# A two-layer hybrid recurrent backbone: the first layer's modulation starts in the mLSTM stage instead of HGRN2, and its weights come through GpSimd's DMA queue

## The chip, the cores and the metric

The kernel runs on one core of one Trainium2 chip. A core has TensorE (PE; its weight loads are a row of their own, PEld), VectorE (DVE), ScalarE (ACT), GpSimd (POOL) and SyncE (SP); the last two here mostly issue transfers or stand idle. The metric is device time in microseconds (us) of one execution; less is better. Times of several runs are given by their median.

## The reference, cut to what matters

Two layers run over 256 context tokens and 1024 latent tokens of width 1024, all in float32. What the change touches is the modulation: a product of one vector per token kind (latent `c`, context `c_ctx`) with a 1024 x 6144 matrix per layer, whose six pieces shift, scale and gate the two sub-layers.

```python
for layer in range(DEPTH):
    mod_l = (jax.nn.silu(c) @ w_ada[layer] + b_ada[layer])[:, None, :]
    mod_c = (jax.nn.silu(c_ctx) @ w_ada[layer] + b_ada[layer])[None, None, :]
    sh1_l, sc1_l, g1_l, sh2_l, sc2_l, g2_l = jnp.split(mod_l, 6, axis=-1)
    sh1_c, sc1_c, g1_c, sh2_c, sc2_c, g2_c = jnp.split(mod_c, 6, axis=-1)
    pl = split_proj(modulate(xl, sh1_l, sc1_l) @ w_in[layer])
    pc = split_proj(modulate(xc, sh1_c, sc1_c) @ w_in[layer])
    mixed = (hgrn2_mixer(pc, pl, lb_all[layer]),
             mlstm_mixer(pc, pl, ml_gate_bias[layer]),
             retention_mixer(pc, pl, rt_decay_logit[layer], rot),
             gla_mixer(pc, pl, gla_w_a[layer], gla_b_a[layer]))
    ...
    xl = xl + g1_l * mixer_out(raw_l, pl, g_heads[layer], w_out[layer])
    xl = xl + g2_l * sq_relu_mlp(modulate(xl, sh2_l, sc2_l), w_ff1[layer], w_ff2[layer])
```

The pieces `sh1` and `sc1` are needed first; `g1`, `sh2`, `sc2` and `g2` only from the output projection on.

## The kernel before

**Stages.** A layer is: the norm and the first projections; the mixers (method `mixers`) in the order GLA, HGRN2 (two pairs of heads), mLSTM (two pairs), retention (two pairs); the output projection (`outproj`); the MLP (`mlp`). Every finished group of chunks of a mixer goes through `finish` (the norm of heads): a matmul at L705, and on DVE the multiplication at L708, by which the stages are told apart below.

**Dense work beside the mixers.** The input projections and gates are products of 128 x 128 weight tiles with all tokens, three matmuls each in reduced precision (L293 to L295 with the weights stationary, L631 to L633 for the values). They stand in a queue (`Fill`). `Fill.along` steps a mixer and the queue in turn by estimated cost; `Fill.until` steps the queue alone until a marked piece is done. The mixers' chains run over DVE, ACT and PE.

**The modulation.** Piece 0 of the first layer (`sh1`, `sc1`) is made at the start on PE. Pieces 1 and 2 come from the generator `ada_part`. It works in eight quarters per piece, each of 256 columns (W = 256). In a quarter, for each of eight slices k of the contraction, a 128 x 256 tile of weights (128 KB) is loaded into a ring of four buffers (L402), and DVE multiplies it with the k-th values of the two vectors and accumulates: L406 for k = 0, L408 for the others, so two DVE instructions per tile and 16 per quarter. Then four small matmuls per quarter (L413) sum over the partitions and DVE adds the bias (L419, and L421 where 1 is added). The two accumulators are used again in the next quarter. In all that is 128 tiles, 256 DVE instructions at L406 and L408, and 16 quarters. The second layer's modulation uses the same generator inside the first layer's MLP with W = 512; it is not changed in substance.

**What sets the order.** `Fill.step` runs the modulation along with the queue: on three of every five steps of the queue it advances the generator by one `yield`. In the kernel before, that begins when HGRN2 begins:

```python
for cost in gen:
    self.n += 1
    if self.also and self.n % 5 in (0, 2, 4):
        next(self.also, None)
    return cost
```

The program is then laid out per engine by a scheduler that may move instructions; each engine runs its own list in order. All loads and stores of this stage, the modulation's weights too, are issued by SP. GpSimd has a few memsets to do (L767, L1289, L1290).

Of the kernel before, what the change touches and what calls it, by code (L numbers as in the profile page):

```python
# [42 lines left out]
class Ring:  # L43
# [4 lines left out]
    def next(self):  # L48
        x = self.items[self.i % len(self.items)]
        self.i += 1  # L50
        return x
# [146 lines left out]
class K:  # L198
# [189 lines left out]
            m = self.mod[:, l, a:a + 8, :]  # L388
            nc.vector.tensor_scalar(m, m, 1.0, None, op0=ALU.add)

    def ada_part(self, l, r, toks, wring, tmp, acc, banks, W):


        nc = self.nc
        one = self.m64[:, 1:2]
        nt, nb = len(toks), W // 128
        for q in range(2048 // W):
            g, h = divmod(q * W, 512)
            A = [b(W) for b in acc[:nt]]
            for k in range(NK):  # L400
                w = wring.next()(W)
                nc.sync.dma_start(w, self.io["w_ada"][l, r, k, :, g, h:h + W])  # L402
                for i, j in enumerate(toks):
                    c = self.cc[:, k, j:j + 1]
                    if k == 0:
                        nc.vector.tensor_scalar(A[i], w, c, None, op0=ALU.mult)  # L406
                    else:
                        nc.vector.scalar_tensor_tensor(A[i], w, c, A[i], op0=ALU.mult, op1=ALU.add)  # L408
                yield
            ps = self.bank(banks().next())  # L410
            for i in range(nt):
                for cb in range(nb):
                    nc.tensor.matmul(ps[:, 2 * cb + i:2 * cb + i + 1], lhsT=A[i][:, 128 * cb:128 * cb + 128], rhs=one,  # L413
                                     start=True, stop=True)
            o = 16 * r + nb * q
            mo = self.mod[:, l, o:o + nb, toks[0]:toks[0] + nt]
            bb = self.bada[:, l, o:o + nb].unsqueeze(2).to_broadcast([128, nb, nt])
            v = ps[:, 0:2 * nb].rearrange("p (c j) -> p c j", j=2)[:, :, 0:nt]
            nc.vector.tensor_tensor(mo, v, bb, op=ALU.add)  # L419
            if (r == 0 and g >= 2) or (r == 2 and g < 2):  # L420
                nc.vector.tensor_scalar(mo, mo, 1.0, None, op0=ALU.add)  # L421
            yield
# [997 lines left out]
    def mixers(self, l, ada):  # L1420
        nc, hp = self.nc, self.heap

        fill = Fill(5)
        sp = self.sp
        gl = self.gl
        gq = [self.copyT(gl, "K", GLK, TBS, 32 ** -0.5), self.copyT(gl, "Q", GLQ, self.otbs)]
        for g in gq:
            g.pre(2)
        m = fill.add(*gq)
        self.turn(sp)  # L1430
        rows = self.ml_rows(sp["sp"])
        next(rows)
        hg = [{"p": p} for p in range(2)]
        ml = [{"p": p} for p in range(2)]
        rt = [{"p": p} for p in range(2)]

        def share(a, b, *names):
            for x in names:
                if x in a:
                    b[x] = a[x]  # L1440

        def ml_dense(p):
            return [self.spill(MLK + p, TBS, 0.125), self.spill(MLQ + p, self.otbs)]


        fill.along(self.feat_gl(gl, sp["sp"]), 1.0)
        hp.free(sp["sp"])
        fill.add(*self.spill_hg(0))
        fill.until(m)
        next(rows, None)  # L1450
        m = fill.add(self.feat_v(0, hg[0]))
        fill.along(self.mix_vec(gl, "gl"), RATIO[0])
        m1 = fill.add(*self.spill_hg(1))
        fill.until(m)

        ao = hp.alloc(1536, True) if l == 0 else None
        if l == 0:
            fill.also = ada([ao.sub(256 * i, 256) for i in range(6)], lambda: self.dbanks)
        self.feat_hg(hg[0])
        share(hg[0], hg[1], "V")  # L1460
        fill.add(*(self.gate(6 + p, GLG + p, True) for p in range(2)))
        fill.along(self.mix_vec(hg[0], "hg"), RATIO[1])
        fill.add(*ml_dense(0))
        fill.until(m1)
        self.feat_hg(hg[1])
        m = fill.add(self.spill_v(1))
        fill.add(self.gate(0, HGG, False), *ml_dense(1))
        fill.along(self.mix_vec(hg[1], "hg"), RATIO[2], fill.done + len(fill.q) - 2)
        hp.free(hg[0]["V"])
        fill.until(m)  # L1470

        V = self.get(ml[0], "V65")(NC, 260)
        for c in range(0, NC, 5):
            nc.sync.dma_start(V[:, c:c + 5, :], self.d_v[:, c:c + 5, :])
        share(ml[0], ml[1], "V65")
        self.rt_setup()
        for p in range(2):
            self.fetch(ml[p], "K", MLK + p, TBS)
            self.fetch(ml[p], "Q", MLQ + p, self.otbs)
            if p == 0:  # L1480
                m = fill.add(self.feat_v(2, rt[0]))
                fill.add(self.gate(1, HGG + 1, False))
            else:
                m = fill.add(*self.feat_rt(rt[0]))
                fill.add(self.gate(2, MLO, False))
            fill.along(self.mix_ml(ml[p]), RATIO[3])
            fill.until(m)
        hp.free(ml[0]["V65"], self.mlN_o, self.mlAE_o)

        share(rt[0], rt[1], "V")  # L1490
        m = fill.add(*self.feat_rt(rt[1]))
        self.rt_tables()
        fill.along(self.mix_rt(rt[0]), RATIO[4])
        last = fill.add(self.gate(3, MLO + 1, False))
        fill.add(self.last_gates(((4, RTG, True), (5, RTG + 1, True))))
        fill.until(m)
        fill.along(self.mix_rt(rt[1]), RATIO[4], last)
        fill.until(10 ** 9)
        if l == 0:
            for _ in fill.also:  # L1500
                pass
            hp.free(ao)
        for x in self.mix_pools:
            x.release()
# [66 lines left out]
def build(ctx, tc, io):  # L1571
    b = K(ctx, tc, io)
    b.setup()
    nc = b.nc
# [14 lines left out]
    for l in range(2):  # L1589
# [3 lines left out]

        def ada(bufs, banks):
            for r in (1, 2):
                yield from b.ada_part(0, r, (0, 1), Ring(bufs[:4]), None, bufs[4:6], banks, 256)
        b.mixers(l, ada)
        b.outproj(l)
        na = 3
# [3 lines left out]
        wring = Ring(cs[:nw])  # L1603
        aring = Ring(zip(cs[nw + nf::2], cs[nw + nf + 1::2]))
        def ada1(bufs, l=l):
            for r in range(3) if l == 0 else ():
                yield from b.ada_part(1, r, (0, 1) if r == 0 else (1,), Ring(bufs[:4]), None, bufs[4:6], lambda: b.banks, 512)
        tmps = b.tmps
        gen = ada1(cs[nw:nw + nf] + tmps.items[4:])

        def filler():
# [126 lines left out]
```

## Time and profile before

| | us |
|---|---|
| median of 3 runs | 3308.24 (3303.61 to 3309.18) |
| the profiled execution | 3300.05 |
| its span from first to last instruction | 3298.2 |
| TensorE busy in the span | 3215.6 (97%) |
| VectorE busy | 2121.8 (64%) |
| ScalarE busy | 1286.1 (39%) |
| GpSimd busy | 10.8 |

The share of busy time is a mean over stages; busy spans of PE are pipelined, so a PE that is busy all the time is not one at its peak. In the trace L708 ends HGRN2 near 555 us, mLSTM's first pair at 613, and retention's last group at 798 us; the output projection follows. In the second layer, which has no modulation beside its mixers, HGRN2 lies between about 2095 and 2283 us.

### The profile page before, as it was taken

The numbers are of one execution on the slowest core, as the hardware profiler recorded it, in microseconds if no ns is written. First come the engines' busy times: TensorE is split into PE (matmuls) and PEld (weight loads), VectorE is DVE, ScalarE is ACT, GpSimd is POOL, SyncE is SP. The second block draws the span as 40 slices with busy tenths as digits, with TensorE's granted clock in tenths as the row PEclk, the third lists the DMA queues.
The fourth block names the chain that finished last, engine by engine and source line by source line (L and its number), as shares of the span: only waits on it lengthen the run. The fifth ranks groups of instructions, "written<-read, shape, count | busy, mean of one in ns | idle before, by whom it ended". The sixth has DMA issues, their size and how long they took to land.

```text
span 3298.2 us, 52930 instructions
## 1 busy us (share of the span) xinstructions
PE 3215.6 (97%) x20936; PEld 2640.0 (80%) x20936; DVE 2121.8 (64%) x4218; ACT 1286.1 (39%) x2665; POOL 10.8 (0%) x41
## 2 busy tenths in 40 slices
PE   7998899999999999999999999999999999999998
PEld 4786688877888888888888678788778888888887
DVE  4778887787666656555655586866756555554546
ACT  4665565445322122121212565765445322222222
POOL 0000000000000000000000000000000000000000
PEclk9999899999999999999999999999999999999999
DMA  5113444434322222222211222333315111111111
GB/s 206 61 50 127 122 133 148 121 101 146 103 80 71 83 65 80 69 64 64 77 39 34 76 66 77 110 114 109 103 58 163 53 50 46 51 51 46 51 48 65
DMA packets 175010, 278.85 MB, mean 85 GB/s; under 512 B 21097, under 2 KB 66825, under 8 KB 174505
## 3 DMA queue, kind: packets, MB, share of 16 engines
q1 hardware_dynamic: 173464, 273.66, 26.5%
q8 instruction: 164, 2.69, 0.3%
q10 hardware_dynamic: 1296, 1.81, 0.2%
q14 instruction: 86, 0.70, 0.1%
HBM read 229.75 MB, written 45.64 MB: 83 GB/s over the span
## 4 chain that ended last, share of the span: by engine, by line
PE 88%; DVE 5%; DMA 3%; ACT 3%; issue 1%; SPq 0%; DVEq 0%; ACTq 0%
PE psum L293 23%; PE psum L294 23%; PE psum L295 23%; PE psum L830 2%; PE psum L600 2%; PE psum L631 2%; PE psum L633 2%; PE psum L632 1%; PE psum L817 1%; PE psum L833 1%; PE psum L1018 1%; PE psum L705 1%; PE psum L1357 1%; PE psum L413 1%; DVE px L990 1%
## 5 line engine op out<-in xcount | busy, mean ns | idle before, releaser
L525 DVE SCALAR_TENSOR_TENSOR x<-psum,st,x 128x512 f32<-128x512 f32 (+1 forms) x648 | 441.3, 690 | 213.2 <-PE psum L295 212.3
L281 ACT ACTIVATE pc<-st 128x512 fp32r<-128x512 f32 x256 | 161.2, 632 | 847.5 <-PE psum L294 808.7
L294 PE MATMUL psum<-pc,pc 128*128 128x512 f32 (+1 forms) x1296 | 475.9, 367 | 0.0
L293 PE MATMUL psum<-pc,pc 128*128 128x512 f32 (+1 forms) x1296 | 475.8, 367 | 0.0
L295 PE MATMUL psum<-pc,pc 128*128 128x512 f32 (+1 forms) x1296 | 473.8, 366 | 0.0
L293 PE MATMUL psum<-Hhi,pc 128*128 128x512 f32 (+1 forms) x1280 | 471.9, 369 | 1.7 <-ACT pc L281 1.5
L294 PE MATMUL psum<-Hlo,pc 128*128 128x512 f32 (+1 forms) x1280 | 471.9, 369 | 0.1
L295 PE MATMUL psum<-Hhi,pc 128*128 128x512 f32 (+1 forms) x1280 | 470.5, 368 | 0.0
L293 PE MATMUL psum<-Hhi,pw 128*128 128x512 f32 (+1 forms) x1192 | 451.0, 379 | 5.7 <-ACT pw L281 2.5
L295 PE MATMUL psum<-Hhi,pw 128*128 128x512 f32 (+1 forms) x1192 | 445.2, 374 | 0.0
L294 PE MATMUL psum<-Hlo,pw 128*128 128x512 f32 (+1 forms) x1192 | 444.8, 373 | 0.0
L504 DVE TENSOR_TENSOR st<-st 128x256 f32<-128x256 f32 (+1 forms) x160 | 101.8, 637 | 301.8 <-ACT pc L503 300.7
L293 PEld LDWEIGHTS psum<-pc,pc 128*128 128x128 f32 x1296 | 244.4, 189 | 43.8 <-DVE x L525 1.3
L295 PEld LDWEIGHTS psum<-pc,pc 128*128 128x128 f32 x1296 | 244.0, 188 | 43.0 <-issue 2.7
L294 PEld LDWEIGHTS psum<-pc,pc 128*128 128x128 f32 x1296 | 244.5, 189 | 41.3 <-issue 2.1
L293 PEld LDWEIGHTS psum<-Hhi,pc 128*128 128x128 f32 x1280 | 241.2, 189 | 43.5 <-ACT pc L281 2.4
L294 PEld LDWEIGHTS psum<-Hlo,pc 128*128 128x128 f32 x1280 | 241.3, 189 | 40.9 <-DVE Hlo L481 0.5
L295 PEld LDWEIGHTS psum<-Hhi,pc 128*128 128x128 f32 x1280 | 241.1, 188 | 40.9 <-DVE pc L282 0.6
L293 PEld LDWEIGHTS psum<-Hhi,pw 128*128 128x128 f32 x1192 | 226.7, 190 | 51.4 <-issue 10.1
L282 DVE TENSOR_TENSOR pc<-st,pc 128x512 fp32r<-128x512 f32 x256 | 175.5, 690 | 137.9 <-ACT pc L281 117.3
L295 PEld LDWEIGHTS psum<-Hhi,pw 128*128 128x128 f32 x1192 | 226.2, 190 | 37.6 <-issue 2.1
L294 PEld LDWEIGHTS psum<-Hlo,pw 128*128 128x128 f32 x1192 | 226.8, 190 | 36.2 <-issue 2.2
(398 smaller groups left out, 4950.4 us busy)
## 6 DMA issues: line engine op xcount, KB each, us to landing
st<-w_ff SPq DMA_DIRECT2D x256, 256.0 KB
st<-w_inT SPq DMA_DIRECT2D x96, 256.0 KB
ph<-w_ada SPq DMA_DIRECT2D x128, 128.0 KB
st<-w_out SPq DMA_DIRECT2D x50, 256.0 KB
pc<-w_ada SPq DMA_DIRECT2D x48, 256.0 KB
st<-w_ada SPq DMA_DIRECT2D x48, 256.0 KB
d_z<-st SPq DMA_DIRECT2D x40, 256.0 KB
ps<-w_ada SPq DMA_DIRECT2D x32, 256.0 KB
```

The source lines that it names most:

```text
L281: nc.scalar.activation(hi, raw, AF.Copy)
L282: (eng or nc.vector).tensor_tensor(lo, raw, F(hi), op=ALU.subtract)
L293: t.matmul(out, lhsT=w[0], rhs=m[0], start=first, stop=False)
L294: t.matmul(out, lhsT=w[0], rhs=m[1], start=False, stop=False)
L295: t.matmul(out, lhsT=w[1], rhs=m[0], start=False, stop=last)
L413: nc.tensor.matmul(ps[:, 2 * cb + i:2 * cb + i + 1], lhsT=A[i][:, 128 * cb:128 * cb + 128], rhs=one, start=True, stop=True)
L504: nc.vector.tensor_tensor(r, r, r, op=ALU.mult)
L525: nc.vector.scalar_tensor_tensor(x, ps, self.mod[:, l, 40 + o, j:j + 1], x, op0=ALU.mult, op1=ALU.add)
L600: t.matmul(ps[:, 0:304], lhsT=h[a], rhs=u[b], start=(k + i == 0), stop=(k == NK - 1 and i == 2))
L631: t.matmul(ps[:, e, :], lhsT=h[0], rhs=u[0], start=(k == 0), stop=False)
L633: t.matmul(ps[:, e, :], lhsT=h[1], rhs=u[0], start=False, stop=(k == NK - 1))
L830: nc.tensor.matmul(o, lhsT=ST[r0:r0 + kd, c, d, :], rhs=qd[d](c)[r0:r0 + kd, :], start=(j == 0), stop=False, tile_position=(r0, 0))
```

## The change

`ada_part` takes the queue on which it loads as an argument. For the first layer's pieces 1 and 2 that is now GpSimd's queue, for the second layer it stays SP's. With W = 256 the generator now yields after every second tile, so each advance issues two loads and four DVE instructions. In `mixers` the buffers are taken and the generator is started after HGRN2's second pair, just before mLSTM. An unused argument goes.

```diff
-    def ada_part(self, l, r, toks, wring, tmp, acc, banks, W):
+    def ada_part(self, l, r, toks, wring, acc, banks, W, queue):
...
                 w = wring.next()(W)
-                nc.sync.dma_start(w, self.io["w_ada"][l, r, k, :, g, h:h + W])
+                queue.dma_start(w, self.io["w_ada"][l, r, k, :, g, h:h + W])
                 for i, j in enumerate(toks):
                     c = self.cc[:, k, j:j + 1]
...
-                yield
+                if W == 512 or k % 2:
+                    yield
...
         fill.until(m)
 
-        ao = hp.alloc(1536, True) if l == 0 else None
-        if l == 0:
-            fill.also = ada([ao.sub(256 * i, 256) for i in range(6)], lambda: self.dbanks)
         self.feat_hg(hg[0])
...
         share(ml[0], ml[1], "V65")
         self.rt_setup()
+        ao = hp.alloc(1536, True) if l == 0 else None
+        if l == 0:
+            fill.also = ada([ao.sub(256 * i, 256) for i in range(6)], lambda: self.dbanks)
         for p in range(2):
...
-                yield from b.ada_part(0, r, (0, 1), Ring(bufs[:4]), None, bufs[4:6], banks, 256)
+                yield from b.ada_part(0, r, (0, 1), Ring(bufs[:4]), bufs[4:6], banks, 256, nc.gpsimd)
...
-                yield from b.ada_part(1, r, (0, 1) if r == 0 else (1,), Ring(bufs[:4]), None, bufs[4:6], lambda: b.banks, 512)
+                yield from b.ada_part(1, r, (0, 1) if r == 0 else (1,), Ring(bufs[:4]), bufs[4:6], lambda: b.banks, 512, nc.sync)
```

The lists of the two programs show where the instructions went. (After L409 the lines of the changed program are one higher: L414 there is L413 before, L420 is L419, L709 is L708, L1304 is L1303, L1290 and L1291 are L1289 and L1290.)

**DVE at the start of HGRN2.** `px` and `ph` are the two memories of the mixers; L882 to L1037 are lines of the HGRN2 mixer, L798 and L802 its chain of states. Before, just behind the L708 that ends GLA:

```order
L990 SCALAR_TENSOR_TENSOR px_0_688<-px_0_688,st 128x512
L408 SCALAR_TENSOR_TENSOR ph_0_251<-ph_0_251,st 128x256 x2
L798 SCALAR_TENSOR_TENSOR ph_0_251<-ph_0_251 128x128
L408 SCALAR_TENSOR_TENSOR ph_0_251<-ph_0_251,st 128x256
L798 SCALAR_TENSOR_TENSOR ph_0_251<-ph_0_251 128x128
L802 SCALAR_TENSOR_TENSOR ph_0_251<-ph_0_251 128x128
L798 SCALAR_TENSOR_TENSOR ph_0_251<-ph_0_251 128x128
L408 SCALAR_TENSOR_TENSOR ph_0_251<-ph_0_251,st 128x256
```

At the same place of the changed program:

```order
L310 SCALAR_TENSOR_TENSOR st<-psum,st 128x512
L723 TENSOR_TENSOR st<-st,psum 128x512
L799 SCALAR_TENSOR_TENSOR ph_0_251<-ph_0_251 128x128
L732 SCALAR_TENSOR_TENSOR st<-st 128x512
L799 SCALAR_TENSOR_TENSOR ph_0_251<-ph_0_251 128x128
L733 TENSOR_TENSOR st<-st 128x512
L799 SCALAR_TENSOR_TENSOR ph_0_251<-ph_0_251 128x128
```

The modulation's L408 is gone from between the mixer's and the dense work's instructions.

**DVE between mLSTM's first and second pair of heads.** L708 (L709 in the changed program) is the first pair's last multiplication; L1303 (L1304) scales the second pair's keys; L282 splits a weight tile, L310 and L651 belong to a gate. Before:

```order
L708 SCALAR_TENSOR_TENSOR st<-st 128x128
L1303 TENSOR_TENSOR px_0_688<-psum,st 128x3x64
L310 SCALAR_TENSOR_TENSOR st<-psum,st 128x256
L1303 TENSOR_TENSOR px_0_688<-psum,st 128x3x64
L419 TENSOR_TENSOR st<-psum,st 128x4
L406 TENSOR_SCALAR ph_0_251<-ph_0_251,st 128x256
L651 TENSOR_TENSOR st<-st 128x256
L421 TENSOR_SCALAR st<-st 128x4
L406 TENSOR_SCALAR ph_0_251<-ph_0_251,st 128x256
L408 SCALAR_TENSOR_TENSOR ph_0_251<-ph_0_251,st 128x256 x2
L798 SCALAR_TENSOR_TENSOR px_0_688<-px_0_688,ph_0_251 128x65
```

In the changed program:

```order
L709 SCALAR_TENSOR_TENSOR st<-st 128x128
L420 TENSOR_TENSOR st<-psum,st 128x4
L406 TENSOR_SCALAR ph_0_251<-ph_0_251,st 128x256 x2
L282 TENSOR_TENSOR pw_0_247<-st,pw_0_247 128x512
L408 SCALAR_TENSOR_TENSOR ph_0_251<-ph_0_251,st 128x256 x8
L1304 TENSOR_TENSOR px_0_688<-psum,st 128x3x64
L408 SCALAR_TENSOR_TENSOR ph_0_251<-ph_0_251,st 128x256 x6
L406 TENSOR_SCALAR ph_0_251<-ph_0_251,st 128x256
L420 TENSOR_TENSOR st<-psum,st 128x4
L406 TENSOR_SCALAR ph_0_251<-ph_0_251,st 128x256
L1304 TENSOR_TENSOR px_0_688<-psum,st 128x3x64
L408 SCALAR_TENSOR_TENSOR ph_0_251<-ph_0_251,st 128x256 x8
```

Before the second pair's keys are scaled, three whole quarters (48 instructions of the modulation, 24 tiles) now stand in DVE's list almost in one piece; the third goes on in the same way behind these rows.

**GpSimd's list in the first layer's mixers.** L1290 and L1291 clear the states of an mLSTM pair, L768 sets a column of ones for its values. Before (L767, L1289, L1290):

```order
L1208 MEMSET ph_0_251 128x16
L767 MEMSET st 128x4 x10
L1289 MEMSET px_0_688 128x65
L1290 MEMSET px_0_688 128x65
L1289 MEMSET px_0_688 128x65
L1290 MEMSET px_0_688 128x65
```

In the changed program:

```order
L1209 MEMSET ph_0_251 128x16
L402 DMA ph_0_251<-w_ada 128x256
L768 MEMSET st 128x4 x10
L1290 MEMSET px_0_688 128x65
L402 DMA ph_0_251<-w_ada 128x256 x4
L1291 MEMSET px_0_688 128x65
L402 DMA ph_0_251<-w_ada 128x256 x22
L1290 MEMSET px_0_688 128x65
L1291 MEMSET px_0_688 128x65
L402 DMA ph_0_251<-w_ada 128x256 x101
```

All 128 loads now stand in GpSimd's list, and some memsets behind them.

Counted over the whole DVE lists, between the multiplications that end the stretches named above (before, then changed): HGRN2 from its first group (289 to 555 us) holds 148 and 7 instructions at L406 and L408; mLSTM's first pair (555 to 613) 16 and 57; up to the second pair's first group (to 644) 14 and 67; the rest of the second pair (to 682) 16 and 34; retention's first pair (to 735) 34 and 56; up to the second pair's first group (to 779) 16 and 35; the rest 0 and 0. The other instructions of DVE in the last six stretches are 112 and 101, 58 and 64, 63 and 71, 71 and 76, 53 and 57, 22 and 20.

## Rows read from the trace of the kernel before

**Rows 1.** The page: busy us by engine; busy tenths and clock in 40 slices.

```profile
PE 3215.6 (97%) x20936; PEld 2640.0 (80%) x20936; DVE 2121.8 (64%) x4218; ACT 1286.1 (39%) x2665; POOL 10.8 (0%) x41
...
PE   7998899999999999999999999999999999999998
PEld 4786688877888888888888678788778888888887
DVE  4778887787666656555655586866756555554546
...
PEclk9999899999999999999999999999999999999999
```

**Rows 2.** Busy time by stretch: HGRN2, mLSTM, retention of layer 0; then layer 1's HGRN2.

```profile
core 0: us, PE busy (x) PEld busy (x) DVE busy (x) ACT busy (x) POOL busy (x), PEclk, DMA share, GB/s
289.00:555.00 266.00, 241.79 (x2339) 198.70 (x2337) 226.10 (x562) 154.41 (x343) 1.28 (x12) 0.94 0.41 127
555.00:613.00 58.00, 56.55 (x484) 49.94 (x483) 44.08 (x128) 27.15 (x84) 0.24 (x2) 1.00 0.44 132
613.00:644.00 31.00, 31.00 (x221) 24.10 (x219) 25.19 (x73) 15.07 (x39) 0.00 (x0) 1.00 0.48 127
644.00:682.00 38.00, 38.00 (x223) 31.06 (x224) 32.04 (x84) 19.23 (x55) 0.00 (x0) 1.00 0.28 86
682.00:735.00 53.00, 53.00 (x361) 40.48 (x360) 42.52 (x107) 21.63 (x50) 0.00 (x0) 1.00 0.36 111
735.00:779.00 44.00, 44.00 (x309) 35.59 (x309) 32.33 (x73) 16.46 (x39) 0.00 (x0) 1.00 0.18 52
779.00:798.00 19.00, 19.00 (x129) 15.05 (x128) 10.39 (x23) 11.50 (x29) 0.00 (x0) 1.00 0.45 144
...
2095.00:2283.00 188.00, 186.33 (x1876) 152.80 (x1874) 132.53 (x282) 119.12 (x251) 1.29 (x12) 1.00 0.34 109
```

**Rows 3.** The same view of L408 alone, the modulation's accumulation on DVE.

```profile
289.00:555.00 266.00, 58.38 (x131) 0.94 0.41 127
555.00:613.00 58.00, 6.30 (x14) 1.00 0.44 132
613.00:644.00 31.00, 5.59 (x12) 1.00 0.48 127
```

**Rows 4.** Stretches of 10 us in HGRN2 with a low clock.

```profile
310.00:320.00 10.00, 2.16 (x64) 1.74 (x64) 10.00 (x21) 3.43 (x7) 0.00 (x0) 0.59 0.39 128
320.00:330.00 10.00, 8.50 (x62) 6.90 (x63) 7.40 (x20) 3.98 (x7) 0.00 (x0) 0.73 0.14 44
360.00:370.00 10.00, 10.00 (x108) 9.14 (x108) 7.16 (x19) 4.18 (x9) 0.00 (x0) 0.68 0.26 83
380.00:390.00 10.00, 5.29 (x25) 3.79 (x25) 7.73 (x20) 5.32 (x12) 0.00 (x0) 0.67 0.64 185
390.00:400.00 10.00, 9.56 (x71) 7.59 (x70) 6.89 (x17) 7.02 (x14) 0.00 (x0) 0.82 0.59 185
```

**Rows 5.** Timelines of DVE and SP: start, us, engine, line, idle before and its end.

```profile
616.23 0.17 DVE L419 TENSOR_TENSOR st<-psum,st 128x4 f32<-128x4 f32 x1 [1.59 <-PE psum L413]
...
741.08 3.33 DVE L408 SCALAR_TENSOR_TENSOR ph<-ph,st 128x256 f32<-128x256 f32 x8
...
741.19 2.71 SPq L402 DMA_DIRECT2D ph<-w_ada  x4
...
744.58 1.28 DVE L408 SCALAR_TENSOR_TENSOR ph<-ph,st 128x256 f32<-128x256 f32 x3 [0.17 <-DMA ph<-w_ada]
```

**Rows 6.** Waits of SP's queue from 280 to 760 us: us, times, longest.

```profile
SPq L402 <- DVE ph L408: 77.3, 63, 9.6
...
SPq L402 <- DVE ph L406: 22.7, 10, 7.8
```

## The prediction

> **What bounds the kernel now.** I read the page first: PE is busy in 97% of the span, and the only slices of the row PE with an 8 behind the start lie where the row DVE has its 8s and 7s and where PEclk drops [rows 1]. So nearly all the kernel runs at PE's pace, and the mixers of layer 0 are where another engine interferes. The second view is busy time by stretch, cut at the L708 that ends each stage [rows 2]. In HGRN2 (289 to 555 us) PE stands idle for 266 - 241.8 = 24.2 us and its clock averages 0.94; DVE is busy for 226.1 us, 85%. From 555 to 798 us PE is busy nearly throughout at clock 1.00, and DVE for 186.5 of 243 us, 77%. Layer 1's HGRN2 is the useful comparison: no modulation beside it, DVE at 132.5 of 188 us (70%), PE idle for only 1.7 us, clock 1.00. HGRN2 is thus bound by PE when DVE has room, and by DVE when it hasn't. The third view finds the modulation in it: 58.4 us of L408 lie in HGRN2, and little per stretch later [rows 3]. The fourth is HGRN2 in steps of 10 us: DVE is busy for all of 310 to 320 while PE does 2.2 us; after such a gap the granted clock lies at 0.59 to 0.82 of full in five of these steps, a mix of the levels 2.4 and 1.2 GHz [rows 4].
>
> **What the change removes from HGRN2.** 141 of its 148 DVE instructions at L406 and L408 go (the lists). At 58.4/131 = 0.45 us each [rows 3] that is 63 us, so DVE has about 163 us to do instead of 226. What can be won is PE's: the idle 24.2 us, and what the low clock costs. Of the latter I take busy time times (1 - clock) for the five steps of [rows 4]: 0.9 + 2.3 + 3.2 + 1.7 + 1.7 = 9.8 us. Some idle time stays, as in layer 1, 0.9% or 2 us. HGRN2 would take 266 - 24.2 - 9.8 + 2 = 234 us, and DVE would be at 163/234 = 70%, exactly layer 1's share, which supports it. **Gain 32 us**; at the most 34, and at the least 24, if the chains of the mixer and not DVE's load made part of the idle time. PE's list in the stretch changes by two things that about cancel: the 72 small matmuls at L413 leave, 66 dense matmuls come in from later.
>
> **What it adds from 555 us on.** The same work now stands in 243 us instead of 509. A back-to-back modulation instruction costs DVE 3.33/8 = 0.41 us [rows 5]; another DVE instruction some 0.33 us, (44.1 - 7)/112 in the first of these stretches [rows 2, 3]. With the counts of the lists DVE then has to do:
>
> - 555 to 613: 44.1 + 41 x 0.41 - 11 x 0.33 = 57.3 us
> - 613 to 644: 25.2 + 53 x 0.41 + 6 x 0.33 = 48.9
> - 644 to 682: 32.0 + 18 x 0.41 + 8 x 0.33 = 42.0
> - 682 to 735: 42.5 + 22 x 0.41 + 5 x 0.33 = 53.2
> - 735 to 779: 32.3 + 19 x 0.41 + 4 x 0.33 = 41.4
> - 779 to 798: 10.4 less two instructions, 9.7
>
> That is 252 us for stretches that last 243 now. So DVE becomes the bound from 555 to 779 us. How full can it be? It reached 10.00 of 10 us once and 85% over HGRN2 [rows 2, 4]. The true share lies between. I take 0.91, nearer to the middle than to the mean of HGRN2, since the modulation's instructions wait for nothing but weights.
>
> **The block between mLSTM's pairs** needs its own term. Three quarters stand nearly in one piece there, 24 tiles, and the second pair's chain begins behind them. The ring has four buffers, so a tile is issued when the tile four before it is used up. In [rows 5] four loads are issued from 741.19 on, right as DVE begins a run of eight, and DVE runs dry and gets the first of these at 744.58: 3.4 us from issue to use. A turn of the ring is then 3.4 + 0.82 (one tile's two instructions) = 4.2 us for four tiles, 1.05 us per tile against 0.82 of DVE work. The block takes 24 x 1.05 = 25.3 us instead of 19.7. The hand-over at a quarter's end, DVE to L413 and back (1.59 us in [rows 5]), is hidden under the ring, which goes on filling; without that cover it would be up to 3 x 1.6 us more. This price is one of SP's queue; GpSimd's does not occur in the trace for a load, so I bound it: not below the 3.4 us of the row (any saving would be in the issue, which is not part of it), and not above twice that. I take the row.
>
> **The sum.** At a share of 0.91: 57.3/0.91 = 63.0; the block 25.3 and the rest (48.9 - 19.7)/0.91 = 32.1, together 57.4; 42.0/0.91 = 46.2; 53.2/0.91 = 58.5; 41.4/0.91 = 45.5; and 16 for the last, which has less dense work left and is bound by PE. Together 286.6 us instead of 243: **a loss of 43.6 us**. Net: +43.6 - 32 = **+11.6 us**. The profiled execution takes 3300.05 us and would become 3312; it lies 8.2 us below the median, so against 3308.24 I expect **3320 us**.
>
> **What I cost at nothing.** SP loses 128 issues and its waits for the ring, 77.3 + 22.7 us [rows 6]. Loads of dense weights stood behind these waits, but PE was busy from 555 on and in HGRN2 was short of DVE, not of weights; the cover is the dense work already loaded. Should weights have been late in HGRN2, that is part of the 24.2 us already counted. GpSimd has 10.8 us of work in the whole span [rows 1], so 128 issues find room. Behind its waiting loads stand the memsets L1290 and L1291 of the states, for which DVE's chain at L798 and L802 waits: the second one of the first pair stands behind the fifth load, which waits for the first tile's use. DVE's list has that use ahead of the chain, so the memset is late by one turn of the ring at most, 4.2 us, and I count nothing. The end of the modulation stays where it was, before retention's last two groups; the output projection sees no difference.
>
> The Trainium skill (DMA: Bandwidth & Descriptors, SWDGE vs HWDGE vs iDMA) says that descriptors of GpSimd's transfers are written by software, and puts the first byte (Latency and other measured facts) near 1 us against 0.6 us for SP's. By that the turn of the ring would be an estimated 0.4 us longer, 2.4 us for the block's 24 tiles, and the sum 3322 us; no row here shows such a load.
>
> **The rivals.**
>
> 1. *Faster: DVE takes it all in without gaps.* Place: 555 to 779 us. With DVE's share at 1.00 and a ring that never runs dry these stretches take 57.3 + 48.9 + 45 + 53.2 + 43 + 16 = 263 us (45 and 43 are PE's need in the third and fifth), a loss of 20, net -12: 3296 us. It decides from a share of 0.955 up: then 223.1/0.955 + 25.3 + 16 = 275 us, the loss is 32 and eats up the gain exactly (223.1 is the sum above without the block and the last stretch). For it: the full 10 us of [rows 4]. Against it: no stage holds over 85%, and mLSTM's chains pass through DVE and wait for PE and ACT in between. Chance 0.17.
> 2. *No change within 0.2% (6.6 us, about what a measurement of this kernel can tell).* The same mechanism with a share from about 0.935 to 0.975, or 0.91 with a smaller excess in the block because PE's dense work hides it. 3302 to 3314 us. Chance 0.25.
> 3. *Much slower: GpSimd's loads take twice as long.* A turn of the ring of 6.8 + 0.8 us is 1.9 us per tile; the block takes 45.6 us, 20 more, and other runs of the modulation in retention perhaps 5 more. Net +32 to +37: 3340 to 3345 us. The page's account of software descriptors would make this more likely. Against it: the other 104 tiles have 2.2 us each, so only runs suffer. Chance 0.15.
> 4. *It doesn't do what it says* is excluded by the lists: HGRN2 loses the work, GpSimd has the loads.
>
> **Numbers.** My forecast, DVE as the bound at a share of 0.85 to 0.935, has a chance of 0.43; its own range is 3314 us to 3337 us (at 0.85: 223.1/0.85 + 41.3 = 303.8 us, a loss of 60.8, net +29). Faster has rival 1, 0.17; the same rival 2, 0.25; slower my forecast and rival 3, 0.58. The range of 8 in 10 reaches from 3298 us, just inside rival 1, to 3343 us, inside rival 3.
>
> **What the new profile would show.** Right: no L408 before 520 us; HGRN2's L708 near 522 instead of 555 us, with PE idle for a few us only and a clock of 1.00; DVE busy at some 0.9 from there to the end of the first retention pair; PE idle for 15 us or more between mLSTM's pairs, waiting for DVE's L1304 behind a run of L408, with waits of L408 for its weights. Wrong in the first step: HGRN2 still takes over 245 us, so it was chains or weights. Wrong in the second: the stretch from HGRN2's end to retention's end lasts under 275 us, because PE's dense list runs on while DVE is behind, or DVE stays above 0.95. Wrong in the price of the queue: L408 waits for weights over 20 us in all.

## The result, and the profile after

The changed kernel takes 3341.82 us (median of 4 runs, 3334.19 to 3346.7) against 3307.5 us before: ratio 1.0103, 95% interval 1.0081 to 1.0125, 34 us slower. The forecast was 3320 us with slower at 0.58. The profiled execution takes 3339.83 us.

The page of the changed kernel, busy us by engine and tenths in 40 slices:

```profile
PE 3240.0 (97%) x20936; PEld 2658.6 (80%) x20936; DVE 2126.1 (64%) x4218; ACT 1282.5 (38%) x2665; POOL 79.7 (2%) x169
...
PE   7999999789999999999999999999999999999998
...
PEclk9999998789999999999999999999999999999999
```

Beside [rows 1], PE's two 8s of HGRN2 are gone, and a 7 and an 8 with a lower clock stand four slices later, in mLSTM and at the start of retention. The shares of PE, DVE and ACT over the span are the same to a per cent: they can't show this change.

Busy time by stretch, cut as in [rows 2] at the last multiplication of each stage (L709 now): HGRN2's two pairs; mLSTM's first pair in two halves; up to the second pair's first group; its rest; retention's three stretches.

```profile
core 0: us, PE busy (x) PEld busy (x) DVE busy (x) ACT busy (x) POOL busy (x), PEclk, DMA share, GB/s
290.49:409.42 118.93, 117.66 (x1125) 95.41 (x1123) 92.28 (x212) 79.14 (x175) 1.52 (x9) 1.00 0.35 112
409.42:525.36 115.94, 113.99 (x1214) 96.08 (x1211) 80.04 (x190) 70.70 (x164) 3.22 (x10) 1.00 0.31 99
525.36:555.72 30.36, 28.25 (x230) 24.57 (x229) 22.32 (x70) 8.30 (x27) 6.42 (x12) 0.94 0.36 112
555.72:600.61 44.89, 35.14 (x161) 27.18 (x160) 33.33 (x91) 15.04 (x46) 9.56 (x20) 0.67 0.36 112
600.61:657.38 56.77, 43.69 (x276) 35.39 (x277) 46.67 (x131) 13.67 (x34) 17.52 (x34) 0.75 0.47 147
657.38:707.90 50.52, 48.39 (x278) 39.34 (x276) 41.57 (x110) 22.98 (x66) 9.64 (x18) 1.00 0.31 97
707.90:772.59 64.69, 53.95 (x345) 41.53 (x346) 52.67 (x135) 21.11 (x48) 15.02 (x28) 0.87 0.31 101
772.59:818.95 46.36, 44.90 (x308) 35.51 (x307) 39.51 (x94) 17.00 (x40) 7.51 (x14) 1.00 0.32 100
818.95:835.20 16.25, 16.11 (x108) 12.53 (x107) 9.32 (x22) 9.92 (x25) 0.00 (x0) 1.00 0.52 164
```

HGRN2 takes 235 us instead of 266, with PE idle for 3 us and its clock at 1.00. From its end to retention's end it is 310 us instead of 243. PE's account of these seven rows closes: it is idle for 39.4 us, and busy time times (1 - clock) gives another 31 us; before, both together were 1.5 us, and the difference of 69 us accounts for the loss of 67. No engine is full there: DVE is at 74 to 82% in the three rows in which PE loses most, and at 85% at most.

L408 alone, which answers to [rows 3], in HGRN2, mLSTM's first pair, and up to its second pair's first group:

```profile
290.49:525.36 234.87, 1.99 (x5) 1.00 0.33 106
525.36:600.61 75.25, 22.51 (x52) 0.78 0.36 112
600.61:657.38 56.77, 23.91 (x57) 0.75 0.47 147
```

Busy time in steps of 10 us, from the second half of mLSTM's first pair on:

```profile
570.00:580.00 10.00, 8.14 (x28) 5.89 (x28) 7.18 (x17) 5.36 (x16) 0.96 (x2) 0.53 0.22 67
580.00:590.00 10.00, 7.47 (x27) 5.87 (x27) 6.73 (x21) 1.09 (x3) 2.92 (x7) 0.50 0.44 140
590.00:600.00 10.00, 6.18 (x21) 4.26 (x21) 8.31 (x29) 3.05 (x10) 3.06 (x6) 0.50 0.43 138
600.00:610.00 10.00, 8.61 (x37) 7.42 (x37) 7.80 (x22) 2.58 (x7) 4.69 (x10) 0.59 0.47 147
610.00:620.00 10.00, 3.51 (x28) 3.01 (x28) 8.44 (x24) 1.04 (x2) 4.85 (x10) 0.58 0.41 135
```

The lower level, 1.2 GHz, which before stood in HGRN2 [rows 4], stands here now for most of these 50 us. The dense matmuls have moved too, the products for the values most, here at L632 (L633 now), before and then after, in HGRN2's pairs and the second half of mLSTM's first pair:

```profile
289.10:427.74 138.64, 0.00 (x0) 0.00 (x0) 0.89 0.39 121
427.74:554.91 127.17, 29.36 (x103) 19.65 (x103) 1.00 0.44 134
583.35:613.20 29.85, 9.20 (x31) 5.69 (x30) 1.00 0.50 150
```

```profile
290.49:409.42 118.93, 10.18 (x36) 6.69 (x36) 1.00 0.35 112
409.42:525.36 115.94, 27.01 (x93) 17.68 (x93) 1.00 0.31 99
555.72:600.61 44.89, 0.85 (x3) 0.49 (x3) 0.67 0.36 112
```

Summed over all six lines of dense matmuls, HGRN2's first pair holds 469 instead of 344, its second 496 instead of 548, and the second half of mLSTM's first pair 34 instead of 121. So HGRN2 has taken over 73 dense matmuls. Not all of mLSTM is short of them: the stretch that loses most, up to the second pair's first group, holds 87 instead of 78, and the whole of mLSTM 362 instead of 392.

Timelines of DVE and PE at the start of retention's first pair, which answer to [rows 5]:

```profile
708.77 2.85 DVE L408 SCALAR_TENSOR_TENSOR ph<-ph,st 128x256 f32<-128x256 f32 x7
...
712.17 1.80 DVE L408 SCALAR_TENSOR_TENSOR ph<-ph,st 128x256 f32<-128x256 f32 x4
...
713.63 1.87 PE L414 MATMUL psum<-st,ph 128*128 128x1 f32 x8 [6.51 <-DVE ph L408]
718.23 1.12 PE L818 MATMUL psum<-px,ph 128*64 128x64 f32 x16 [2.73 <-DVE ph L1135]
...
722.89 0.79 PE L293 MATMUL psum<-Hhi,pw 128*128 128x512 f32 x1 [2.28 <-DVE st L310]
```

DVE works off eleven accumulations, PE waits with a quarter's small matmuls at the head of its in-order list, and the dense work stands behind them. Each wait ends on DVE.

GpSimd's queue: its loads, and its waits, in the place of SP's [rows 6]:

```profile
L402 POOL DMA_DIRECT2D ph<-w_ada x128: 536/536/683, 338.5 to 795.1; - x128
...
  DVE ph L408: 6.6, 12
...
DMA to landing us min/median/max: 2.5/2.7/5.3
```

```profile
POOL ph L402 <- DVE ph L408: 106.2, 86, 12.4
...
POOL ph L402 <- DVE ph L406: 44.6, 11, 9.3
```

A load takes 0.54 us of GpSimd and lands 2.7 us after its issue; DVE waited for weights 6.6 us in twelve times. GpSimd waits for the ring, and little waits for GpSimd.

### The profile page after: what moved, and what is told of

It reads as the page before. It is cut to its first block, busy times and chain, and to the rows that moved or that the text cites. A ratio compares the mean times of both kernels' runs of the same rounds, so it can differ in the third digit from the quotient of the medians.

```text
span 3338.1 us, 53007 instructions
## 1 busy us (share of the span) xinstructions
PE 3240.0 (97%) x20936; PEld 2658.6 (80%) x20936; DVE 2126.1 (64%) x4218; ACT 1282.5 (38%) x2665; POOL 79.7 (2%) x169
## 4 chain that ended last, share of the span: by engine, by line
PE 82%; DVE 5%; issue 5%; DMA 3%; ACT 3%; POOL 1%; SPq 0%; POOLq 0%; DVEq 0%; ACTq 0%
PE psum L293 22%; PE psum L294 21%; PE psum L295 21%; PE psum L601 2%; PE psum L831 2%; PE psum L632 2%; PE psum L634 2%; PE psum L633 1%; PE psum L1019 1%; PE psum L834 1%; PE psum L818 1%; POOL ph L402 1%; PE psum L706 1%; PE psum L1358 1%; DMA ph<-w_ada 1%
## 5 line engine op out<-in xcount | busy, mean ns | idle before, releaser
L282 DVE TENSOR_TENSOR pc<-st,pc 128x512 fp32r<-128x512 f32 x256 | 175.4, 689 | 138.0 <-ACT pc L281 117.4
```

The costliest lines, as they stand in the source:

```text
L282: (eng or nc.vector).tensor_tensor(lo, raw, F(hi), op=ALU.subtract)
```

## The experiments

Ratios are to the kernel before on the same chip. The theory ahead of the first runs was that of the prediction: the modulation's work on VectorE is too dense from mLSTM on. Rival: GpSimd's queue.

**One part alone, one part undone.**

```diff
 late_sp (of the changed kernel)
-                yield from b.ada_part(0, r, (0, 1), Ring(bufs[:4]), bufs[4:6], banks, 256, nc.gpsimd)
+                yield from b.ada_part(0, r, (0, 1), Ring(bufs[:4]), bufs[4:6], banks, 256, nc.sync)
 early_gp (of the kernel before)
-                nc.sync.dma_start(w, self.io["w_ada"][l, r, k, :, g, h:h + W])
+                nc.gpsimd.dma_start(w, self.io["w_ada"][l, r, k, :, g, h:h + W])
 late_reuse (of the changed kernel)
+                if W == 512 or (r == 1 and q == 0 and k < 4):
                     queue.dma_start(w, self.io["w_ada"][l, r, k, :, g, h:h + W])
```

Expected of `late_sp`: 

> The changed kernel with one part undone: the modulation's 128 loads go back to SP's queue; the late start and the yield after two tiles stay. Theory of VectorE's load (its work now stands in mLSTM and retention, which chains through VectorE, TensorE and ScalarE can't fill over 0.8): the queue does not matter, 3342 us within 6 either way. Rival, GpSimd's queue is the price: the turn of the ring of four buffers gets shorter and some 25 us come back, 3317 us.

Expected of `early_gp`: 

> The kernel before with one part of the change alone: the loads come through GpSimd's queue; the start in HGRN2 and the yield after every tile stay as before. Theory of VectorE's load: no change, 3308 us within 4. Rival, GpSimd's queue: VectorE runs dry more often in HGRN2, where it bounds, and the kernel takes 3320 us or more.

Expected of `late_reuse`: 

> The changed kernel with the modulation's loads left out but for the first four tiles, which all quarters then use again, so the output is not the reference's; all 256 instructions on VectorE and the small matmuls stay. Theory of VectorE's load: only the waits for weights go, 8 us on VectorE and not all on the path, 3334 to 3341 us. Rival, GpSimd's queue or the ring of four: 25 us or more come back, 3317 us or less.

Measured: `late_sp` 3337.43 us, ratio 1.0092 (1.0071 to 1.0113); `early_gp` 3315.04 us, 1.0015 (1.0005 to 1.0024); `late_reuse` 3344.41 us, 1.0103 (1.0088 to 1.0118). Without 124 of the 128 loads nothing comes back: loads, ring and landing times are free, the late block too. In the order of the kernel before, the queue alone costs about 5 us, 1 us more than the theory allowed; in the late order the intervals of the two queues overlap (1.0092 and 1.0103). The rivals' 12 us and 25 us do not come: they fall.

**Half of the modulation's VectorE work, none of it, and no small matmuls.**

```diff
 late_onetok (of the changed kernel)
-                yield from b.ada_part(0, r, (0, 1), Ring(bufs[:4]), ...
+                yield from b.ada_part(0, r, (1,), Ring(bufs[:4]), ...
 no_mod (of the changed kernel)
-            fill.also = ada([ao.sub(256 * i, 256) for i in range(6)], lambda: self.dbanks)
+            nc.gpsimd.memset(self.mod[:, 0, 16:48, :], 0.5)
+            fill.also = iter(())
 late_nomm (of the changed kernel)
-                for cb in range(nb):
+                for cb in range(nb if W == 512 else 0):
                     nc.tensor.matmul(ps[:, 2 * cb + i:2 * cb + i + 1], ...
+            if W == 256:
+                ps = A[0]
```

Expected of `late_onetok`: 

> The changed kernel with half of the modulation's work on VectorE: only the latent's vector is multiplied and the context's column of pieces 1 and 2 is set to a constant, so the output is not the reference's; all 128 loads stay, by the same queue and ring. Theory of VectorE's load: 128 instructions of 0.41 us go, 52 us, VectorE falls from 245 to some 193 us between HGRN2's end and retention's end, and the stretch, which takes 310 us in the changed kernel, goes back to TensorE's pace, 245 to 258 us: 3280 to 3290 us in all. Rival, GpSimd's queue: the ring still turns at the queue's pace, the stretch stays over 285 us, 3320 us or more.

Expected of `no_mod`: 

> The changed kernel without the modulation's pieces 1 and 2: no loads, no VectorE work, no small matmuls; the two pieces are set to a constant, so the output is not the reference's. It gives the floor against which both places of the work are priced. Theory of VectorE's load: HGRN2 stays at 235 us, and from its end to retention's end TensorE's pace is back, 238 to 246 us instead of 310: 3270 to 3280 us. Rival, the mixers' own chains in the changed order make the loss: the stretch stays over 270 us, 3302 us or more.

Expected of `late_nomm`: 

> The changed kernel without the 64 small matmuls that end the quarters: the addition of the bias reads the first accumulator instead, so the output is not the reference's; loads and all 256 instructions on VectorE stay. In the late trace these matmuls stand in TensorE's list and wait there for VectorE, 15.5 us in the matmul row, and VectorE waits 10.3 us for them in turn. Theory of TensorE's in-order wait (dense work stands behind the small matmuls, TensorE idles and its clock falls): 12 to 25 us come back, 3317 to 3330 us. Rival, VectorE's load alone with its own chains: under 8 us, 3334 to 3342 us.

Measured: `late_onetok` 3303.32 us, 0.9985 (0.9972 to 0.9998); `no_mod` 3257.93 us, 0.9843 (0.9822 to 0.9865); `late_nomm` 3328.47 us, 1.0048 (1.0030 to 1.0065). (The four small matmuls per quarter of the program are eight in the trace, so `late_nomm` takes away 128, not the 64 that its expectation counts.)

The run without modulation is the floor, 12 us below its forecast. By stretch, HGRN2's first pair and mLSTM's first pair in two halves:

```profile
291.94:410.98 119.04, 117.73 (x1125) 95.41 (x1123) 92.40 (x211) 79.51 (x175) 0.85 (x8) 1.00 0.35 111
...
526.97:552.78 25.81, 25.81 (x234) 22.04 (x233) 18.49 (x56) 10.85 (x35) 0.00 (x0) 1.00 0.34 96
552.78:583.97 31.19, 30.73 (x228) 25.38 (x228) 23.05 (x64) 18.36 (x49) 0.23 (x2) 1.00 0.45 133
```

Its HGRN2 takes 235.0 us, as in the changed kernel, so the change has taken back there all that the modulation cost. The rest (527.0 to 752.6 us) takes 225.6 us, against 243 before and 310 after. The sums of DVE's busy time in this rest are 150 us (`no_mod`), 186 (before), 198 (`late_onetok`) and 245 (after): 48 us of added work cost 48 in `late_onetok` (273.7 us), and 96 us cost 84 after. Part of that is PE's own work, the small matmuls above all. The time that PE loses, idle or by the low clock, is 3 us in `no_mod`, 41 in `late_onetok` and 71 after, so the 48 us on DVE cost 38 us of it and the 96 us cost 68: 0.7 to 0.8 us per microsecond, at half the load too. The kernel before adds 37 us on DVE and loses only 1.5 us on PE; its 17 us more than `no_mod` are PE's work (754 dense matmuls instead of 667, and small ones). There DVE's work was free, at 77% of this rest, while `late_onetok` pays with DVE at 72%. That goes against the theory as I had put it: a VectorE that is a bound only above some share would have let the halved work through for nothing, at 3280 to 3290 us.

Of `late_nomm` the wait at the start of retention's first pair tells most; its L820 is the changed kernel's L818:

```profile
PE psum L820 <- DVE ph L1137: 10.7, 1, 10.7
```

The 6.5 us that PE waited with the small matmuls, and 2.7 more with L818, are now one wait of 10.7 us for the same late DVE. The time lies within the forecast of the in-order wait, but what came back, 13 us by the medians and 18 by the ratios, is about what the matmuls themselves took: PE's busy time from HGRN2's start to retention's end falls from 502.1 to 485.8 us. The in-order wait was a name for DVE being late, not a cause of its own.

**A third place.** The buffers are taken and the generator starts ahead of HGRN2's second pair, in place of mLSTM.

```diff
 mid_pairs_sp (of late_sp)
+        ao = hp.alloc(1536, True) if l == 0 else None
+        if l == 0:
+            fill.also = ada([ao.sub(256 * i, 256) for i in range(6)], lambda: self.dbanks)
         self.feat_hg(hg[1])
 mid_ones4_sp (of mid_pairs_sp)
-            if self.also and self.n % 5 in (0, 2, 4):
+            if self.also and self.n % 5 in (0, 1, 2, 4):
-                if W == 512 or k % 2:
-                    yield
+                yield
```

Expected of `mid_ones4_sp`: 

> A third place: the modulation begins with HGRN2's second pair of heads, the loads are SP's, it yields after every tile and is advanced on four of five steps. VectorE's list then holds 93 instructions of the modulation in HGRN2's second pair, 28 in the first mLSTM pair, 26 up to the second one's end, 69 and 41 in retention, none later. Theory (the price is made by density, and a stretch at TensorE's pace takes such work for nothing until VectorE is at about 0.83, as HGRN2's second pair before): HGRN2's first pair gains 20 us as in the changed kernel, the second one and mLSTM stay as before, retention's first pair loses a few us: 3285 to 3295 us. Rival, the modulation costs the same wherever it stands: 3308 us.

Expected of `mid_pairs_sp`: 

> As the third place, but with the changed kernel's yield after two tiles on three of five steps: 102 instructions of the modulation in HGRN2's second pair, 55 in mLSTM's first pair, 36 up to the second one's end, 63 in retention's first pair, none in the second. Theory (density): HGRN2's first pair gains 20 us, but mLSTM's first pair loses 10 or more as in the changed kernel, though it has fewer than 57 in its second half: 3293 to 3310 us, behind the finer version. Rival (only the total of VectorE's work up to retention's end counts): the same as the finer version within 4 us.

Measured: `mid_ones4_sp` 3359.57 us, 1.0146 (1.0122 to 1.0170); `mid_pairs_sp` 3363.58 us, 1.0160 (1.0135 to 1.0185). Both miss by 60 us, and density can't be the whole reason: in `mid_ones4_sp` HGRN2's first pair, which holds four instructions of the modulation, all at its end from 415 us on, takes 127 us instead of 119. Row of `mid_ones4_sp` for that pair:

```profile
291.47:418.61 127.14, 101.05 (x943) 78.63 (x942) 88.98 (x207) 74.28 (x164) 0.21 (x2) 0.81 0.29 91
```

Its six lines of dense matmuls count 289 there, not 469, and PE loses 45 us, 26 idle and 19 by the clock. (The second pair, with 104 instructions of the modulation in the trace, loses 46.) DVE's timeline near its end shows a chain with nothing beside it:

```profile
395.95 1.01 DVE L990 SCALAR_TENSOR_TENSOR px<-px,st 128x256 f32<-128x256 f32 x2 [0.69 <-ACT px L988]
397.81 0.29 DVE L975 TENSOR_TENSOR px<-ph 128x128 f32<-128x128 f32 x1 [0.86 <-PE psum L1018]
...
398.79 1.00 DVE L990 SCALAR_TENSOR_TENSOR px<-px,st 128x256 f32<-128x256 f32 x2
400.66 0.30 DVE L1031 COPY_PREDICATED px<-st,psum 128x128 f32<-128x128 int32 x1 [0.86 <-PE psum L1018]
```

DVE, PE and ACT wait for each other in turn, every 3 us. PE is busy for 2.5 and 2.9 of 10 us from 390 to 410, at clock 0.77 and 0.50.

So a second theory: a stretch is slow where the mixer's chain has no dense matmuls left to run beside it, and then everything on DVE ahead of the chain adds to it. Where the dense work lies is the scheduler's choice, and the place of the modulation's buffers may be part of it.

**The buffers' place alone.** The buffers are taken ahead of HGRN2, as in the kernel before, and only the start of the generator moves; `late_keep_sp` loads on SP's queue besides.

```diff
 late_keep (of the changed kernel)
+        ao = hp.alloc(1536, True) if l == 0 else None
         self.feat_hg(hg[0])
...
         self.rt_setup()
-        ao = hp.alloc(1536, True) if l == 0 else None
         if l == 0:
             fill.also = ada([ao.sub(256 * i, 256) for i in range(6)], lambda: self.dbanks)
 mk_ones4_sp (of mid_ones4_sp)
+        ao = hp.alloc(1536, True) if l == 0 else None
         self.feat_hg(hg[0])
...
-        ao = hp.alloc(1536, True) if l == 0 else None
         if l == 0:
             fill.also = ada([ao.sub(256 * i, 256) for i in range(6)], lambda: self.dbanks)
         self.feat_hg(hg[1])
```

Expected of `late_keep`: 

> The changed kernel with one line moved: the buffers of the modulation are taken before HGRN2, as in the kernel before; the generator still starts ahead of mLSTM, yields after two tiles and loads by GpSimd's queue. The scheduler then pulls the work forward: VectorE's list holds 16 instructions of the modulation up to HGRN2's first pair's end, 47 in its second pair, 46 in mLSTM, 45 and 102 in retention. Theory of density, with the place of the buffers as what decides it: HGRN2's first pair keeps 15 to 18 us of its gain, the second pair its TensorE pace, mLSTM is as before, retention's second pair loses 3 to 8 us: 3288 to 3298 us. Rival, the start ahead of mLSTM and the coarse yield make the loss wherever the buffers lie: 3330 us or more.

Expected of `late_keep_sp`: 

> The same with the loads on SP's queue, VectorE's list nearly the same. Theory of density: the queue changes nothing, within 4 us of the run with GpSimd's queue, 3288 to 3298 us. Rival, GpSimd's queue matters once VectorE is not overloaded (128 loads fewer in SP's in-order list, in which the mixers' and the dense weights' loads wait behind them): SP's version is slower by 6 us or more.

Expected of `mk_ones4_sp`: 

> The third place again (start with HGRN2's second pair, SP's queue, one tile per advance, four of five steps), with the buffers taken before HGRN2's first pair. The scheduler pulls part of the work forward: 49 instructions of the modulation up to the first pair's end, 97 in the second, 38 in mLSTM, 30 and 42 in retention. Theory, the buffers' place made the 50 us that this start lost: HGRN2's first pair 130 to 138 us, its second 125 to 130 us instead of 141, mLSTM as before: 3298 to 3310 us. Rival, 93 or more instructions in HGRN2's second pair are over the edge by themselves: that pair stays at 138 us or more, 3320 us or more.

Measured: `late_keep` 3316.42 us, 1.0014 (1.0002 to 1.0026); `late_keep_sp` 3311.01 us, 0.9988 (0.9976 to 1.0001); `mk_ones4_sp` 3305.41 us, 0.9975 (0.9962 to 0.9989). By the ratios, one line moved gives back 29 us of the change's 34, and 57 us of the third place. The last run beats both kernels, by 8 us against the one before; its time lies within its forecast, and HGRN2's pairs take 130 and 133 us. The sizes of the first two were missed by 18 and 13 us: HGRN2's second pair and retention's first pair stay slow, 126 and 65 us. The queue shows once more: 5 us between the first two, as with `early_gp`, and not the 4 us or less of the theory; where these 5 us lie no run shows.

The traces tell what the moved line changed. For three stretches the table has the dense matmuls, the modulation's instructions on DVE, and the us that PE loses (idle, plus busy time times 1 - clock): A is the second half of mLSTM's first pair, B goes from there to the second pair's first group, C is retention's first pair.

| | A | B | C |
|---|---|---|---|
| before | 121, 16, 0.6 | 78, 14, 0.0 | 145, 34, 0.0 |
| `no_mod` | 87, 0, 0.5 | 49, 0, 1.0 | 163, 0, 0.0 |
| `late_onetok` | 88, 19, 2.9 | 67, 32, 14.9 | 96, 27, 11.2 |
| `late_keep` | 55, 18, 8.2 | 83, 22, 0.5 | 125, 56, 17.8 |
| `late_keep_sp` | 22, 19, 13.0 | 82, 23, 1.2 | 125, 56, 17.6 |
| changed | 34, 36, 21.3 | 87, 67, 24.0 | 125, 56, 17.8 |

In `late_keep` HGRN2 holds 966 dense matmuls, as in `no_mod`, against 965 in the changed kernel: that HGRN2 takes them over costs nothing by itself, and the moved line does not undo it. What it moves is the modulation: 85 of its instructions run in HGRN2 instead of 7 (its expectation counted 63), and 77 in mLSTM instead of 161. HGRN2 gets 15 us longer by it and mLSTM 35 us shorter. In B, with about as many dense matmuls, the loss follows the modulation's instructions: 0.5 us with 22, 24.0 with 67. In A four runs have 16 to 19 of them, and the loss rises from 0.6 over 2.9 and 8.2 to 13.0 us as the dense matmuls fall from 121 over 88 and 55 to 22. In `mk_ones4_sp` the moved line does bring dense matmuls back: HGRN2's first pair holds 433 instead of 289, and PE loses 14 us there instead of 45, with 67 instructions of the modulation instead of four.

What keeps the last run from more is the start of retention's first pair, in steps of 6 us:

```profile
687.00:693.00 6.00, 6.00 (x50) 4.64 (x49) 6.00 (x19) 4.12 (x10) 0.00 (x0) 1.00 0.28 82
693.00:699.00 6.00, 2.72 (x36) 2.19 (x34) 5.32 (x15) 3.59 (x11) 0.00 (x0) 0.79 0.61 183
699.00:705.00 6.00, 6.00 (x36) 4.99 (x34) 4.64 (x13) 3.35 (x10) 0.00 (x0) 0.50 0.49 153
705.00:711.00 6.00, 6.00 (x32) 5.74 (x29) 5.79 (x19) 0.18 (x1) 0.00 (x0) 0.50 0.01 3
711.00:717.00 6.00, 6.00 (x26) 4.30 (x24) 4.62 (x10) 0.90 (x2) 0.00 (x0) 0.50 0.63 198
717.00:723.00 6.00, 6.00 (x20) 3.70 (x19) 0.00 (x0) 1.09 (x2) 0.00 (x0) 0.50 0.06 20
723.00:729.00 6.00, 6.00 (x30) 4.64 (x28) 4.34 (x9) 1.32 (x2) 0.00 (x0) 0.94 0.11 44
```

PE is idle for 3.3 us once, and then busy throughout at 0.50 for four steps, 24 us at half its pace: an estimated 12 us lost behind a gap of 3.

**Half of the work to GpSimd.** The context's products and additions of `mk_ones4_sp` go from VectorE to GpSimd.

```diff
 hg2_mk (of mk_ones4_sp)
+                    if W == 256 and i == 0:
+                        if k == 0:
+                            nc.gpsimd.tensor_scalar(A[i], w, c, None, op0=ALU.mult)
+                        else:
+                            t = acc[2](W)
+                            nc.gpsimd.tensor_scalar(t, w, c, None, op0=ALU.mult)
+                            nc.gpsimd.tensor_tensor(A[i], A[i], t, op=ALU.add)
...
-                yield from b.ada_part(0, r, (0, 1), Ring(bufs[:4]), bufs[4:6], banks, 256, nc.sync)
+                yield from b.ada_part(0, r, (0, 1), Ring(bufs[:3]), bufs[3:6], banks, 256, nc.sync)
```

Expected: 

> The run that began with HGRN2's second pair with its buffers taken early (SP's queue, one tile per advance, four of five steps), and in it the context's half of the modulation moved from VectorE to GpSimd: 128 products and 112 additions there, each rounded by itself, with one of the four weight buffers given up for the product. Theory (the price is VectorE's work beside the mixers): 128 instructions of 0.41 us leave VectorE, 52 us; half of the modulation's price of 47 us over the run without it comes back: HGRN2's pairs 120 to 124 us each instead of 130 and 132, retention's first pair 55 instead of 63: 3275 to 3288 us. Rival: GpSimd is slower than the work it takes over (an addition of 128 x 512 took 1.37 us in the trace, so an estimated 0.7 us and as much for the product, 1.4 us per tile, against 0.41 us on VectorE), the small matmuls in TensorE's list and the ring wait for it: 3300 us or more.

Measured: 3330.54 us, 1.0055 (1.0036 to 1.0074), on the rival's side: HGRN2's pairs take 151 and 143 us, only retention's first pair shrinks as forecast, to 53. GpSimd's two lines in this run, and then DVE's accumulation and the costliest line of HGRN2 in it:

```profile
L410 POOL TENSOR_SCALAR ph<-ph,st 128x256 f32<-128x256 f32 x112 | 130.3, 1163 | 126.7 <-DMA ph<-w_ada 119.8
L411 POOL TENSOR_TENSOR ph<-ph 128x256 f32<-128x256 f32 x112 | 96.4, 860 | 9.3
...
L997 DVE SCALAR_TENSOR_TENSOR px<-px,st 128x512 f32<-128x512 f32 (+1 forms) x100 | 77.0, 771 | 8.0 <-ACT px L995 6.1
L415 DVE SCALAR_TENSOR_TENSOR ph<-ph,st 128x256 f32<-128x256 f32 x112 | 68.0, 607 | 2.3 <-DMA ph<-w_ada 1.6
```

The same two lines in `mk_ones4_sp`:

```profile
L408 DVE SCALAR_TENSOR_TENSOR ph<-ph,st 128x256 f32<-128x256 f32 x224 | 98.6, 476 | 0.0
L990 DVE SCALAR_TENSOR_TENSOR px<-px,st 128x512 f32<-128x512 f32 (+1 forms) x100 | 69.2, 694 | 7.8 <-ACT px L988 6.5
```

An accumulation on DVE takes 607 ns instead of 476, and DVE's busy time over the mixers is 417.5 us instead of 410.3 although 128 instructions have left it. The Trainium skill (SBUF — State Buffer, Who interferes with whom) says that a VectorE instruction with two inputs in SBUF contends with a GpSimd instruction that reads SBUF. These rows agree, 607 against 476 ns; no run here separates that from the ring of three buffers and the changed order.

## Why the prediction was right, and where not

1. *HGRN2 gains 32 us, 266 to 234.* Measured 31.0, 265.8 to 234.9, clock 1.00. Right, and `no_mod` confirms that the whole excess was the modulation's.
2. *DVE has 252 us to do from 555 us on.* Measured 245.4. Right.
3. *The block between mLSTM's pairs, 57.4 us.* Measured 56.8, but not for its reason: `late_reuse`, which has no loads to wait for, takes 60.0 us there. PE is idle for 13 us there, of which it waits 6.9 for L408 ahead of a quarter's small matmuls and 4.8 for L1304; the ring doesn't matter. The agreement in size is luck.
4. *DVE's share of 0.91.* This is the term that was mis-sized: 286.6 us forecast for the stretches, 309.8 measured, a share of 0.80 over all but the last. mLSTM's first pair has 12 of the missing 23 us (75.2 against 63.0), retention's first pair 6 (64.7 against 58.5). `late_onetok` shows that it is wrong in kind: PE loses 0.7 to 0.8 us per microsecond of DVE work at half the load as well, and before it lost 1.5 us in all with DVE at 77%. What stands in its place is a chain through DVE, PE and ACT that waits behind runs of the modulation in DVE's list, partly at 1.2 GHz.
5. *What I cost at nothing: "PE was busy from 555 on", and dense matmuls that come into HGRN2 cancel against L413 there.* This is the step behind the wrong term: PE was not busy from 555 us on, it lost 71 us to gaps and to the low clock. The sum counts DVE's work over a share; it has no term for a chain that waits behind the modulation, nor for the clock. The half clock, which I counted in HGRN2 as a gain of 9.8 us, was not counted where the gaps would go; it took 31 us. The dense matmuls cancel in HGRN2, and one stretch of mLSTM missed them, 121 to 34 in the second half of its first pair; but the stretch behind it lost 24 us with more of them than before.
6. *The queue.* Rival 3 has the right time, 3340 us, by a wrong cause: waits for weights were 6.6 us, not over 20, and `late_sp` and `late_reuse` stay at 3337 and 3344 us. Rivals 1 and 2 needed a DVE share of 0.935 or more, or a cheaper block.
7. *The time.* The way was right, slower, but 34 us stand against the 12 of the sum. The measured time lies outside the forecast's own range of 3314 to 3337 us and inside that of 8 in 10 only because rival 3 had stretched it; with that rival's cause refuted, this is luck.

That the late modulation's work on DVE makes the loss is shown: `late_reuse` takes out the loads, `late_nomm` the small matmuls, `late_onetok` half of the work and `no_mod` all. That missing dense work adds to it is argued from the counts, A above all, and from `mid_ones4_sp`, where a pair with next to no modulation slows down with 289 dense matmuls instead of 469; a run that changes the dense work alone was not made. Why the scheduler lays it so when the buffers come late stays open.

## What to carry to other kernels

Price moved work by what runs beside it at the new place: count the filler that is left there, and how long a run of the moved work stands ahead of a chain in an engine's list. A free share on an engine is no room if its instructions stand in a chain; add them to the chain's length, and the low clock behind each gap. Where a scheduler orders the lists, taking a buffer later can cost more than the start of the work that uses it: here one such line held 78 instructions back from a place where they were cheaper.

## What was not expected of the hardware

One gap of 3.3 us on PE stood ahead of 24 us at half clock with PE busy throughout. GpSimd took 1.16 us for a product of 128 x 256 and 0.86 us for an addition beside DVE, and DVE's accumulation took 28% longer in that run. GpSimd's queue delivered 128 KB in a median of 2.7 us, and 128 such loads on it, in place of SP's, cost the kernel about 5 us in two pairs of runs that differ in it alone.
